# A two-layer hybrid trunk on one core: the norms' last pass put on VectorE, statistics' DMAs issued by ScalarE, leftover attention pieces handed out at another spacing

## The chip, the core and the metric

The kernel runs on one core of a Trainium2 chip, with its five engines: TensorE (PE in the profile, with its weight loads as PEld), VectorE (DVE), ScalarE (ACT), GpSimd (POOL) and SyncE (SP), which issues most DMAs. The metric is the device time of one execution in microseconds; the time of a kernel is the median of its runs.

## The reference, cut to what matters

Two layers over a sequence of 1024 positions and a width of 1024. Layer 0 mixes tokens by dilated sliding-window attention in three head groups, layer 1 by a gated linear recurrence (HGRN2). Behind each mixer stands an MLP. Each of the four sub-layers ends in a LayerNorm of alpha * x + sublayer(x).

```python
def dilated_attention_mixer(x, w_in, w_out):
    proj = (x @ w_in).reshape(B, S, N_GROUPS, 3, ATTN_HEADS, ATTN_HEAD_DIM)
    for g, (window, dilation) in enumerate(((128, 1), (512, 4), (2048, 16))):
        q = rotary(proj[:, :, g, 0], pos)
        k = rotary(proj[:, :, g, 1], pos)
        o, lse = dilated_window_attention(q, k, proj[:, :, g, 2], window, dilation)
        outs.append(o)
        lses.append(lse)
    wts = jax.nn.softmax(jnp.stack(lses, axis=0), axis=0)
    o = jnp.einsum('gbsh,gbshe->bshe', wts, jnp.stack(outs, axis=0))
    return o.reshape(B, S, ATTN_HEADS * ATTN_HEAD_DIM) @ w_out

def squared_relu_mlp(x, w_up, w_down):
    return jnp.square(jax.nn.relu(x @ w_up)) @ w_down

def reference(x, ...):
    for i in range(2):
        y = dilated_attention_mixer(x, ...) if i == 0 else hgrn2_mixer(x, ...)
        x = layer_norm(DEEPNORM_ALPHA * x + y, ln_mix_g[i], ln_mix_b[i])
        y = squared_relu_mlp(x, ffn_w_up[i], ffn_w_down[i])
        x = layer_norm(DEEPNORM_ALPHA * x + y, ln_ffn_g[i], ln_ffn_b[i])
    return x
```

## The kernel before

**Products.** All large products run in split precision: an operand is written as a high part (a rounded copy, made by ACT, line 137) and a low part (the rest, subtracted by DVE, line 138), and three matmuls add up high x high, low x high and high x low. In the names, h and l at the end mark the two parts (woh and wol of the output weights, wh and wl of the recurrent layer's, aoh and aol of the attention's output, d3s of a factor in the MLP).

**Attention.** The projections to q, k and v are computed by 252 steps, in 12 groups of 21, each a product of quarter matrices in a scheme with seven instead of eight products. A group feeds two units; a unit is one pair of heads in one of the three head groups (dilations 16, 4 and 1; eight pairs in all). Unit work is cut in pieces: rotary (line 472 copies by DMA to rot), score products and exponentials (lines 502 to 516), transposes of the probabilities (526, copied to pts by ACT at 529), value products (541, copied to og at 549 or 552). The pieces are put in slots between later projection steps, by tables of numbers; within this part PE and DVE run in exactly the order that the program writes, and so does every engine in its own queue.

**Statistics.** Each unit leaves row maxima and sums in a tile, stats. The function `combine_tr` turns it round on PE (mpt, line 566), copies it to sr (ACT, 569), writes sr to a small array in DRAM, mdram (572), and reads that back in another layout into ml (578 for dilation 1, 581 for the others, where the positions are reordered). Once all three units of a pair are there, `combine` works out the softmax weights over the groups on DVE and ACT (595 to 608), splits them into fh and fl (612, 614), and writes these by six small DMAs into frow (619). `combine_mul` spreads frow over the partitions by a matmul (fb, 629) and weighs the three outputs og with it (630 to 633).

**What is left at the end.** The pieces of the last group, and those whose slots lie past step 252, are packed in 22 lists. `outproj_ln`, which multiplies the attention's output by its output weights and forms the norm, calls `tick()` behind each set of three matmuls; a tick hands out lists in proportion, so that all are out after `ticks` of them (53 for the attention). The first `stage_a` products use the pairs that are ready (nka of them). Earlier pairs lie in DRAM and are read back into onr (875). z is the running sum of a tile of 128 positions, loaded from x at line 911 and finished at 937.

**Norm.** `ln_math` runs over one z tile (128 positions x 1024): statistics (196, 198), subtract the mean and multiply by g (199), the inverse root on small columns (201 to 206), then multiply by it (213, ACT) and add b (214, POOL). The 24 norms of the first three sub-layers end so; the eight of the last one use the branch at 208 to 212, which does both on DVE by halves and stores. The result goes to transposes on PE (lnpt, 223), whose banks ACT and DVE empty into the next operand (233, 234, 291).

There are three PSUM banks for product sums (pmm) and two for transposes. Behind the attention, a scheduler of the framework sets the order on each engine, and inserts the waits; each engine then runs its own queue in order.

Of the kernel before, what the change touches and what calls it, by code (L numbers as in the profile page):

```python
# [9 lines left out]
F32 = mybir.dt.float32  # L10
F32R = mybir.dt.float32r
U8 = mybir.dt.uint8
AF = mybir.ActivationFunctionType
ALU = mybir.AluOpType
AX = mybir.AxisListType

P = 128
# [5 lines left out]
DIL = (1, 4, 16)  # L23
# [39 lines left out]
def trunk_kernel(  # L63
# [24 lines left out]
    nc = tc.nc  # L88
# [16 lines left out]
    act = nc.scalar.activation  # L105
# [87 lines left out]
    def ln_math(z, gB, bB, store=None):  # L193
        st = small([P, 2, 6], "lnst")
        for i in range(2):
            nc.vector.bn_stats(st[:, i], z[:, i * 512:(i + 1) * 512])
        mv = small([P, 2], "lnmv")
        nc.vector.bn_aggr(mv, st)
        nc.vector.scalar_tensor_tensor(z, z, mv[:, 0:1], gB, op0=ALU.subtract, op1=ALU.mult)
        w = small([P, 4], "lnw")  # L200
        act(w[:, 0:1], mv[:, 1:2], AF.Ln, bias=eps_ln)
        act(w[:, 1:2], w[:, 0:1], AF.Exp, scale=-0.5)
        r = w[:, 1:2]
        nc.vector.tensor_scalar(w[:, 2:3], mv[:, 1:2], LN_EPS, r, op0=ALU.add, op1=ALU.mult)
        nc.vector.tensor_scalar(w[:, 2:3], w[:, 2:3], r, -0.5, op0=ALU.mult, op1=ALU.mult)
        nc.vector.tensor_scalar(w[:, 3:4], w[:, 2:3], 1.5, r, op0=ALU.add, op1=ALU.mult)
        if store is not None:
            for i in range(2):
                c = slice(i * 512, i * 512 + 512)
                nc.vector.scalar_tensor_tensor(z[:, c], z[:, c], w[:, 3:4], bB[:, c], op0=ALU.mult, op1=ALU.add)  # L210
                nc.sync.dma_start(store[:, c], z[:, c])
            return
        act(z, z, AF.Copy, scale=w[:, 3:4])  # L213
        nc.gpsimd.tensor_add(z, z, bB)  # L214

    def z_tr(z):

# [104 lines left out]
    def attention(pre, hc):  # L322
# [121 lines left out]
        frow = U("frow", F32R)  # L444
# [119 lines left out]
        def combine_tr(pr, g, slot, ml):  # L564
            pt = bank("pt", "mpt")
            nc.tensor.transpose(pt[:, 0:P], allS, ident)
            q = slice(slot * 32, slot * 32 + 32)
            sr = small([P, P], "sr", 2)
            act(sr[q], pt[q, 0:P], AF.Copy)
            yield  # L570
            md = mdram[pr, g]
            nc.sync.dma_start(md.rearrange("w h (b q) -> (w h b) q", q=P), sr[q])
            yield

            d = DIL[g]
            for w in range(2):
                if d == 1:
                    nc.sync.dma_start(ml[:, w, 0, :], md[w].rearrange("h (i n) -> (h i) n", n=P))
                else:
                    for h in range(2):  # L580
                        nc.sync.dma_start(
                            ml[8 * h:8 * h + 8, w, g, :].rearrange("i (r n) -> i r n", r=d),
# [3 lines left out]
        def combine(pr, ml):  # L586
# [27 lines left out]
            v.tensor_sub(fl, l, fh.bitcast(F32))  # L614
            yield
            for g in range(NG):
                for i, f in enumerate((fh, fl)):
                    r = 4 * g + 2 * i
                    nc.sync.dma_start(frow[r:r + 2, :].bitcast(F32).rearrange("h (i t) -> h i t", t=P),
                                      f[:, g, :].bitcast(F32))  # L620
            yield

        def combine_mul(pr, og, hb):
# [141 lines left out]
        for n in range(len(seq)):  # L765
# [27 lines left out]
            if n % 21 == 14:  # L793
# [25 lines left out]
                                tail[a][0].remove(f)  # L819
        order.__exit__()  # L820
        (ra, ca, sa, _), (rb, cb, sb_, mx) = tail
        done = [f for n in sorted(fill) for f in fill[n]]
        mine = [[ra[0]], [rb[0], rb[1]], [ra[1]], [ca[0], rb[2]], [ca[1]], [cb[0]], [ca[2]], [cb[1]], [ca[3]], [cb[2]],
                [ca[4]] + sa, [cb[3]], [ca[5]], [cb[4]] + sb_, [cb[5]], mx[:1], mx[1:3], mx[3:5], [],
                mx[5:7], mx[7:10], mx[10:]]
        lists = [done[k:k + 1] + (mine[k] if k < len(mine) else []) for k in range(max(len(done), len(mine)))]
        return oN, lists


# [60 lines left out]
    def outproj_ln(pr, oN, fill, resid, gB_ap, bB_ap, keep):  # L890
# [26 lines left out]
        parts = {}  # L917
        total = max(len(fill), 1)
        count = [0, 0]
        ticks = 3 * nka + 5 * 7  # L920

        def tick():
            count[0] += 1
# [840 lines left out]
```

## Time and profile before

| | us |
|---|---|
| three runs | 2829.97, 2828.23, 2829.61 |
| median | 2829.61 |
| profiled execution | 2828.98 |
| its span, first to last instruction | 2827.2 |
| PE busy in it | 2766.7 |
| DVE, ACT, POOL busy | 2069.0, 1450.8, 122.9 |

The granted TensorE clock was 0.997 of full over the span. A row of the timeline reads: start, duration, engine, line, operation, output<-inputs, shape, count of equal rows merged; in brackets the engine's idle time before it and what ended that. A row of the groups has the count, the busy time in all and the mean in nanoseconds of one, and the idle time before it. By forms, a row has the shortest, median and longest duration in nanoseconds.

### The profile page before, as it was taken

The page shows a single profiled execution, that of the slowest core. Times are in us where ns is not written, and L with a number is a line of the kernel's source. Part 1 is how long each engine was busy: PE and PEld are TensorE (multiplying, and loading weights), DVE is VectorE, ACT ScalarE, POOL GpSimd, SP SyncE. Part 2 cuts the span into 40 slices and gives each one's busy share as a digit, 9 for nine tenths or more (in the row PEclk, how much of TensorE's full clock was granted, in tenths as well). Part 3 has the DMA queues.
Part 4 walks back from the last instruction along what each step waited for, and adds up shares of the span by engine and source line. Part 5 has one row for each costly group of instructions (what it writes and reads, how often), then busy time and mean ns, then how long its engine had stood idle before and what let it go on. Part 6 is the DMA issues. An engine that isn't in the chain of part 4 may idle for free.

```text
span 2827.2 us, 40131 instructions
## 1 busy us (share of the span) xinstructions
PE 2766.7 (98%) x14280; PEld 2229.3 (79%) x14280; DVE 2069.0 (73%) x3830; ACT 1450.8 (51%) x3105; POOL 122.9 (4%) x68
## 2 busy tenths in 40 slices
PE   8999999999999989999999999999999999999998
PEld 6777777777777757888878887788887788878887
DVE  7768777777877767786686876565667787678687
ACT  5455555655555555544454444555553644454443
POOL 0000000000000003100000011111102200000000
PEclk9999999999999999999999999999999999999999
DMA  7766665766666523464494752011132355475654
GB/s 286 255 187 208 191 207 173 217 201 198 201 200 220 168 83 134 146 224 160 152 324 127 260 178 98 8 60 60 61 112 104 128 211 176 154 278 188 221 176 130
DMA packets 204936, 485.27 MB, mean 172 GB/s; under 512 B 29376, under 2 KB 43712, under 8 KB 204736
## 3 DMA queue, kind: packets, MB, share of 16 engines
q1 hardware_dynamic: 204736, 482.72, 51.1%
q8 instruction: 112, 1.84, 0.3%
q14 instruction: 88, 0.72, 0.1%
HBM read 362.82 MB, written 94.24 MB: 162 GB/s over the span
## 4 chain that ended last, share of the span: by engine, by line
PE 90%; DVE 5%; ACT 2%; DMA 1%; issue 1%; POOL 0%; SPq 0%; DVEq 0%; POOLq 0%; ACTq 0%
PE pmm L669 8%; PE pmm L671 8%; PE pmm L670 8%; PE pup L1118 7%; PE pup L1116 7%; PE pup L1117 7%; PE pdy L1268 4%; PE pdy L1264 4%; PE pdy L1267 4%; PE s L502 3%; PE pdx L1267 3%; PE pmm L171 3%; PE pdx L1268 3%; PE pmm L173 3%; PE pdx L1264 3%; PE pmm L172 3%
## 5 line engine op out<-in xcount | busy, mean ns | idle before, releaser
L669 PE MATMUL pmm<-xh,H 128*128 128x512 f32 x1008 | 408.5, 405 | 13.2 <-ACT H L432 9.6
L671 PE MATMUL pmm<-xh,H 128*128 128x512 f32 x1008 | 396.5, 393 | 0.2 <-DVE H L440 0.2
L670 PE MATMUL pmm<-xl,H 128*128 128x512 f32 x1008 | 396.0, 393 | 0.0
L669 PEld LDWEIGHTS pmm<-xh,H 128*128 128x128 f32 x1008 | 190.8, 189 | 54.1 <-ACT H L432 9.6
L671 PEld LDWEIGHTS pmm<-xh,H 128*128 128x128 f32 x1008 | 190.4, 189 | 42.6 <-DVE H L440 1.1
L670 PEld LDWEIGHTS pmm<-xl,H 128*128 128x128 f32 x1008 | 191.1, 190 | 36.6
L516 ACT ACTIVATE p<-p,stats 128x128 f32<-128x128 f32 (+1 forms) x384 | 168.3, 441 | 90.7 <-DVE stats L513 89.3
L1264 PE MATMUL pdy<-dT,dS 128*128 128x512 f32 x512 | 199.2, 389 | 0.0
L1267 PE MATMUL pdy<-dT,dS 128*128 128x512 f32 x512 | 199.2, 389 | 0.0
L1268 PE MATMUL pdy<-dT,dS 128*128 128x512 f32 x512 | 199.2, 389 | 0.0
L513 DVE CUSTOM_DVE_ANT_0 p<-s,mask 128x128 f32<-128x128 f32 (+1 forms) x384 | 113.3, 348 | 66.5 <-PE s L502 56.8
L137 ACT ACTIVATE dS<-dr 128x512 fp32r<-128x512 f32 x192 | 119.5, 622 | 73.1 <-PE pdy L1268 36.6
L171 PE MATMUL pmm<-f0nh,wh 128*128 128x512 f32 x384 | 153.1, 399 | 0.0
L173 PE MATMUL pmm<-f0nh,wl 128*128 128x512 f32 x384 | 150.1, 391 | 1.7 <-DVE wl L138 1.6
L172 PE MATMUL pmm<-f0nl,wh 128*128 128x512 f32 x384 | 149.8, 390 | 0.0
L138 DVE TENSOR_TENSOR dS<-dr,dS 128x512 fp32r<-128x512 f32 x192 | 135.4, 705 | 16.2 <-ACT dS L137 14.3
L214 POOL TENSOR_TENSOR z<-z,bB 128x1024 f32<-128x1024 f32 x24 | 58.6, 2444 | 1673.1 <-ACT z L213 1663.0
L529 ACT ACTIVATE pts<-ppt 128x256 f32<-128x256 f32 (+1 forms) x192 | 85.4, 474 | 61.1 <-PE ppt L526 59.0
L137 ACT ACTIVATE dT<-hold 128x512 fp32r<-128x512 f32 x128 | 80.0, 625 | 69.0 <-DVE hold L1243 28.4
L1077 ACT ACTIVATE H<-wc 128x512 fp32r<-128x512 f32 x128 | 77.2, 625 | 73.3 <-DVE wc L1070 43.9
L1267 PEld LDWEIGHTS pdy<-dT,dS 128*128 128x128 f32 x512 | 96.1, 188 | 20.0
L1268 PEld LDWEIGHTS pdy<-dT,dS 128*128 128x128 f32 x512 | 96.1, 188 | 20.0
(396 smaller groups left out, 6946.6 us busy)
## 6 DMA issues: line engine op xcount, KB each, us to landing
xh<-xtd SPq DMA_DIRECT2D x110, 512.0 KB
xl<-xtd SPq DMA_DIRECT2D x110, 512.0 KB
dr<-hd SPq DMA_DIRECT2D x192, 256.0 KB
dr<-in_w_down_dram SPq DMA_DIRECT2D x128, 256.0 KB
rot<-e SPq DMA_DIRECT2D x192, 128.0 KB
wa<-in_w_up_dram SPq DMA_DIRECT2D x48, 512.0 KB
wb<-in_w_attn_dram SPq DMA_DIRECT2D x36, 512.0 KB
wa<-in_w_attn_dram SPq DMA_DIRECT2D x33, 512.0 KB
```

The costliest lines, as they stand in the source:

```text
L137: act(hi, raw, AF.Copy)
L171: nc.tensor.matmul(o, wh[:, k], xs.h(k), start=k == 0, stop=False)
L172: nc.tensor.matmul(o, wh[:, k], xs.l(k), start=False, stop=False)
L173: nc.tensor.matmul(o, wl[:, k], xs.h(k), start=False, stop=k == NK - 1)
L669: nc.tensor.matmul(o, wh, hi[k // 2][:, c], start=begin and k == 0, stop=False, skip_group_check=True)
L670: nc.tensor.matmul(o, wh, lo[k // 2][:, c], start=False, stop=False, skip_group_check=True)
L671: nc.tensor.matmul(o, wl, hi[k // 2][:, c], start=False, stop=end and k == 3, skip_group_check=True)
L1116: nc.tensor.matmul(o, wh, xf.h(b, k), start=begin and k == 0, stop=False, skip_group_check=True)
L1117: nc.tensor.matmul(o, wh, xf.l(b, k), start=False, stop=False, skip_group_check=True)
L1264: nc.tensor.matmul(o[q], h, T_[:, L], start=begin, stop=False, skip_group_check=True)
L1267: nc.tensor.matmul(o[q], h, T_[:, R], start=False, stop=False, skip_group_check=True)
L1268: nc.tensor.matmul(o[q], l, T_[:, L], start=False, stop=end, skip_group_check=True)
```

## The change

It has four parts. The norm's multiply and add become one DVE instruction. In `combine_tr` the write of sr is issued by ACT; for dilation 1 the rows go from sr to ml directly, by two DMAs. In `combine` the three DMAs of fh are issued by ACT, and those of fl stay on SP. The leftover pieces keep their slots' spacing up to a point (slots 0 to 4 as they were, later ones closer), the transposes of the statistics come one list ahead of their DMAs, and the lists are spread over 45 ticks for the attention, not 53.

```diff
@@ ln_math
-        act(z, z, AF.Copy, scale=w[:, 3:4])
-        nc.gpsimd.tensor_add(z, z, bB)
+        nc.vector.scalar_tensor_tensor(z, z, w[:, 3:4], bB, op0=ALU.mult, op1=ALU.add)
@@ combine_tr
-            q = slice(slot * 32, slot * 32 + 32)
+            q0 = slot * 32
             sr = small([P, P], "sr", 2)
-            act(sr[q], pt[q, 0:P], AF.Copy)
+            act(sr[q0:q0 + 32], pt[q0:q0 + 32, 0:P], AF.Copy)
             yield
             md = mdram[pr, g]
-            nc.sync.dma_start(md.rearrange("w h (b q) -> (w h b) q", q=P), sr[q])
+            d = DIL[g]
+            if d == 1:
+                for w in range(2):
+                    nc.scalar.dma_start(ml[:, w, 0, :], sr[q0 + 16 * w:q0 + 16 * w + 16])
+            else:
+                nc.scalar.dma_start(md.rearrange("w h (b q) -> (w h b) q", q=P), sr[q0:q0 + 32])
             yield
 
-            d = DIL[g]
-            for w in range(2):
-                if d == 1:
-                    nc.sync.dma_start(ml[:, w, 0, :], md[w].rearrange("h (i n) -> (h i) n", n=P))
-                else:
+            if d > 1:
+                for w in range(2):
                     for h in range(2):
                         nc.sync.dma_start(
                             ml[8 * h:8 * h + 8, w, g, :].rearrange("i (r n) -> i r n", r=d),
...
@@ combine
             for g in range(NG):
-                for i, f in enumerate((fh, fl)):
+                for i, (f, eng) in enumerate(((fh, nc.scalar), (fl, nc.sync))):
                     r = 4 * g + 2 * i
-                    nc.sync.dma_start(frow[r:r + 2, :].bitcast(F32).rearrange("h (i t) -> h i t", t=P),
-                                      f[:, g, :].bitcast(F32))
+                    eng.dma_start(frow[r:r + 2, :].bitcast(F32).rearrange("h (i t) -> h i t", t=P),
+                                  f[:, g, :].bitcast(F32))
@@ attention, the lists
-        done = [f for n in sorted(fill) for f in fill[n]]
+        done = {}
+        for n in sorted(fill):
+            k = n - len(seq)
+            done.setdefault(k if k < 5 else min(k - 3, 6 + (k - 8) // 2 + (k - 8) % 2), []).extend(fill[n])
-                [ca[4]] + sa, [cb[3]], [ca[5]], [cb[4]] + sb_, [cb[5]], mx[:1], mx[1:3], mx[3:5], [],
+                [ca[4]] + sa[:1], sa[1:] + [cb[3]], [ca[5]], sb_[:1] + [cb[4]], sb_[1:] + [cb[5]], mx[:1], mx[1:3], mx[3:5], [],
-        lists = [done[k:k + 1] + (mine[k] if k < len(mine) else []) for k in range(max(len(done), len(mine)))]
+        lists = [done.get(k, []) + (mine[k] if k < len(mine) else []) for k in range(max(max(done) + 1, len(mine)))]
@@ outproj_ln
-        ticks = 3 * nka + 5 * 7
+        ticks = 3 * nka + 5 * 7 - (8, 0)[pr.mixer]
```

How the order moves is shown at three places. The line numbers of the changed program differ by one to four from those before. First ACT at the end of the attention, where the last pair's statistics leave. Before:

```order
L529 ACTIVATE pts<-ppt 128x512
L569 ACTIVATE sr<-mpt 32x128
L516 ACTIVATE p,stats<-p,stats 128x256 x4
L529 ACTIVATE pts<-ppt 128x512 x2
L552 ACTIVATE og<-o 128x2x256
L137 ACTIVATE aoh<-onr 128x512
L529 ACTIVATE pts<-ppt 128x512 x2
L569 ACTIVATE sr<-mpt 32x128
L137 ACTIVATE aoh<-onr 128x512
L549 ACTIVATE og<-o 128x512
L137 ACTIVATE woh<-wor 128x512 x2
L137 ACTIVATE aoh<-onr 128x512
```

The same place with the change:

```order
L568 ACTIVATE sr<-mpt 32x128
L576 DMA mdram<-sr 32x128
L528 ACTIVATE pts<-ppt 128x512
L515 ACTIVATE p,stats<-p,stats 128x256 x4
L528 ACTIVATE pts<-ppt 128x512 x2
L137 ACTIVATE woh<-wor 128x512 x2
L137 ACTIVATE aoh<-og 128x512
L551 ACTIVATE og<-o 128x2x256
L568 ACTIVATE sr<-mpt 32x128
L528 ACTIVATE pts<-ppt 128x512
L574 DMA ml<-sr 16x128 x2
L528 ACTIVATE pts<-ppt 128x512
```

The last sr now stands ahead of both last pts copies, its two DMAs stand in ACT's queue, and a high part made from og (no load needed) comes ahead of it, where two made from the loaded onr stood.

Second SP, over the same time, from the last long row of frow writes to the load of the norm's weights. Before:

```order
L581 DMA ml<-mdram 8x16x8 x4
L864 DMA wor<-in_w_attn_out_dram 128x512 x2
L911 DMA z<-in_x_dram 128x1024
L875 DMA onr<-ond 128x512
L572 DMA mdram<-sr 32x128
L581 DMA ml<-mdram 8x4x32 x4
L875 DMA onr<-ond 128x512
L911 DMA z<-in_x_dram 128x1024
L572 DMA mdram<-sr 32x128
L864 DMA wor<-in_w_attn_out_dram 128x512 x2
L578 DMA ml<-mdram 16x128 x2
L875 DMA onr<-ond 128x512 x4
```

With the change, from a little earlier:

```order
L915 DMA z<-in_x_dram 128x1024 x3
L471 DMA rot<-e 32x1024 x8
L620 DMA frow<-fl 2x8x128 x3
L582 DMA ml<-mdram 8x16x8 x4
L868 DMA wor<-in_w_attn_out_dram 128x512 x2
L582 DMA ml<-mdram 8x4x32 x4
L915 DMA z<-in_x_dram 128x1024
L879 DMA onr<-ond 128x512 x2
L915 DMA z<-in_x_dram 128x1024
L868 DMA wor<-in_w_attn_out_dram 128x512 x2
L620 DMA frow<-fl 2x8x128 x3
L879 DMA onr<-ond 128x512 x4
```

The writes of mdram and the reads for dilation 1 are gone from SP. The first three z loads stand ahead of the rotary copies and the frow writes (before, one frow write stood ahead of them), and the last four onr loads stand behind the last frow writes.

Third DVE where the first MLP ends and the recurrent layer's products begin, the second-last norm of that stage (f0nl is the low part of the next stage's operand). Before:

```order
L204 TENSOR_SCALAR lnw<-lnmv,lnw 128x1
L234 TENSOR_TENSOR f0nl<-lnpt,f0nh 128x2x128
L205 TENSOR_SCALAR lnw<-lnw 128x1
L206 TENSOR_SCALAR lnw<-lnw 128x1
L138 TENSOR_TENSOR d3s<-d_16021,d3s 128x256
L234 TENSOR_TENSOR f0nl<-lnpt,f0nh 128x2x128 x2
```

With the change:

```order
L204 TENSOR_SCALAR lnw<-lnmv,lnw 128x1
L233 TENSOR_TENSOR f0nl<-lnpt,f0nh 128x2x128
L205 TENSOR_SCALAR lnw<-lnw 128x1
L138 TENSOR_TENSOR d3s<-d_15999,d3s 128x256
L206 TENSOR_SCALAR lnw<-lnw 128x1
L233 TENSOR_TENSOR f0nl<-lnpt,f0nh 128x2x128
L213 SCALAR_TENSOR_TENSOR z<-z,lnw,bB 128x1024
```

The norm's last pass (L213) now stands in DVE's queue two rows behind lnw, ahead of the f0nl rows that follow.

## The prediction

> **What bounds the kernel now.** The page comes first.
>
> ```profile
> span 2827.2 us, 40131 instructions
> PE 2766.7 (98%) x14280; PEld 2229.3 (79%) x14280; DVE 2069.0 (73%) x3830; ACT 1450.8 (51%) x3105; POOL 122.9 (4%) x68
> ```
>
> PE is busy for 2766.7 of 2827.2 us, so some 60 us is all that any edit outside the matmuls can win, and a change in ACT's or DVE's total counts only where PE waits for them. I therefore went through PE's timeline for every wait over a quarter of a microsecond and kept those that the edited code can touch. They lie at three seams, where one stage's norms and the next stage's first products overlap: attention to its output projection (about 975 to 1095 us), the first MLP to the recurrent layer (1726 to 1752), and the second output projection (2173 to 2180).
>
> ```profile
> 985.13 0.50 PE L183 MATMUL pmm<-woh,aoh 128*128 128x512 f32 x1 [1.51 <-DVE z L937]
> 1041.47 0.74 PE L183 MATMUL pmm<-woh,aoh 128*128 128x512 f32 x1 [3.62 <-ACT aoh L137]
> 1051.98 1.19 PE L629 MATMUL fb<-frow,bsel 128*128 128x512 f32 x2 [2.46 <-DMA frow<-fh]
> 1093.25 1.10 PE L223 MATMUL lnpt<-ident,z 128*128 128x128 f32 x8 [0.47 <-issue]
> ...
> 1727.43 0.50 PE L1268 MATMUL pdx<-dT,d3s 128*128 128x512 f32 x1 [1.25 <-DVE d3s L138]
> 1736.19 0.63 PE L223 MATMUL lnpt<-ident,z 128*128 128x128 f32 x4 [2.14 <-DVE f0nl L234]
> 1751.11 0.50 PE L173 MATMUL pmm<-f0nh,wl 128*128 128x512 f32 x1 [1.57 <-DVE wl L138]
> ...
> 2173.91 1.10 PE L223 MATMUL lnpt<-ident,z 128*128 128x128 f32 x8 [0.90 <-issue]
> 2179.86 1.10 PE L223 MATMUL lnpt<-ident,z 128*128 128x128 f32 x8 [0.97 <-issue]
> ```
>
> The brackets add up to 14.9 us. The first four belong to the first seam, the next three to the second, the last two to the third.
>
> **Part 1: the norm's last pass.** It removes 24 ACT multiplies and 24 POOL additions and adds 24 DVE instructions that read two SBUF tensors.
>
> ```profile
> L213 ACT ACTIVATE z<-z,lnw x24: 1138/1152/1157, 1066.7 to 2202.5; 128x1024 f32<-128x1024 f32 x24
> L199 DVE SCALAR_TENSOR_TENSOR z<-z,lnmv,gB x32: 1265/1284/3417, 1063.8 to 2820.3; 128x1024 f32<-128x1024 f32 x32
> L214 POOL TENSOR_TENSOR z<-z,bB 128x1024 f32<-128x1024 f32 x24 | 58.6, 2444 | 1673.1 <-ACT z L213 1663.0
> L199 DVE SCALAR_TENSOR_TENSOR z<-z,lnmv,gB 128x1024 f32<-128x1024 f32 x32 | 48.7, 1522 | 0.5
> ```
>
> The trace has no full-width instruction like the added one, but L199 is of its form, with the same shape and kinds of operands. I take its median, 1.28 us, with 1.27 (its fastest) and 1.52 (its mean) as the ends. Total on DVE: 24 x 1.28 = 30.7 us. ACT loses 24 x 1.15 = 27.6 us, and one norm's chain becomes 1.15 + 2.44 - 1.28 = 2.3 us shorter.
>
> What does the removed POOL addition cost others? Look at the second seam.
>
> ```profile
> 1722.34 4.75 POOL L214 TENSOR_TENSOR z<-z,bB 128x1024 f32<-128x1024 f32 x2 [47.42 <-ACT z L213]
> 1724.82 2.89 DVE L138 TENSOR_TENSOR d3s<-d,d3s 128x256 fp32r<-128x256 f32 x2
> 1733.63 2.08 DVE L138 TENSOR_TENSOR d3s<-d,d3s 128x256 fp32r<-128x256 f32 x1
> 1746.37 1.15 ACT L213 ACTIVATE z<-z,lnw 128x1024 f32<-128x1024 f32 x1 [1.41 <-DVE lnw L206]
> 1747.60 2.38 POOL L214 TENSOR_TENSOR z<-z,bB 128x1024 f32<-128x1024 f32 x1 [11.28 <-ACT z L213]
> 1748.56 2.50 DVE L138 TENSOR_TENSOR wl<-wr,wh 128x1024 fp32r<-128x1024 f32 x1 [2.23 <-ACT wh L137]
> L138 DVE TENSOR_TENSOR d3s<-d,d3s x64: 372/419/2560, 1677.2 to 2815.0; 128x256 fp32r<-128x256 f32 x64
> L138 DVE TENSOR_TENSOR wl<-wr,wh x24: 1202/1226/3051, 1741.6 to 2072.2; 128x1024 fp32r<-128x1024 f32 x24
> ```
>
> Two d3s subtractions that take 0.42 each by the median took 2.89 together while POOL added; one took 2.08; wl took 2.50 instead of 1.23, with POOL's 1747.60 row running across its start. Each time the next PE row is one of the three waits of that seam. So POOL's addition holds up DVE's subtractions, and the waits 1.25 + 2.14 + 1.57 = 4.96 us hang on it (wl's also on L213, which stood 1.15 us ahead of wh on ACT). What is late next is the new instruction itself, now in DVE's queue ahead of the same d3s and f0nl. The first event shows the slack: the excess was 2.89 - 0.84 = 2.05 and PE waited 1.25, so 0.80 was covered. A new pass of 1.28 can leave 1.28 - 0.80 = 0.48 uncovered at d3s and again at f0nl; wl's split runs after wh on ACT, which covers it. I take 4.96 - 0.96 = **4.0 us** gained (ends 2.6, with 0.48 lost five times over, and 5.0).
>
> Third seam and the row at 1093.25: the transposes wait, marked "issue", for a bank that ACT must first empty, and ACT stood in L213.
>
> ```profile
> 2172.18 1.14 ACT L213 ACTIVATE z<-z,lnw 128x1024 f32<-128x1024 f32 x1
> ```
>
> That copy (1.14 us) goes, and each of the three waits (0.90, 0.97, 0.47) is shorter than it: **2.3 us** (ends 0, if the transposes then wait for z on DVE, and 2.3).
>
> Where DVE is already full, its added time could show.
>
> ```profile
> 1060.00:1080.00 20.00, 19.63 (x86) 15.93 (x87) 19.82 (x39) 6.24 (x13) 7.58 (x3) 1.00 0.13 52
> ```
>
> Columns after the length: PE, PEld, DVE, ACT, POOL. DVE is busy 19.82 of 20 us and PE still 19.63, so PE lives off three pmm banks. About six norms finish in this stretch and the ten microseconds behind it: 6 x 1.28 = 7.7, less the 3.42 - 1.28 = 2.1 that the slowest L199 loses to POOL, is 5.5 more on DVE at worst. I take **0.6 lost** (ends 0 and 5.5), since 19.63 against 19.82 says that PE follows DVE only loosely.
>
> A rule to weigh here. SBUF — State Buffer in the Trainium skill (the engine and DMA sides of SBUF, under its diagram) has GpSimd and a DVE instruction with two SBUF inputs share one port pair as an exclusive lock for the whole instruction. The single meetings agree (2.08 for 0.42, against POOL's 2.4). Taken for all 24, the rule would let DVE win back up to 58.6 us for 30.7 paid, and the 0.6 would be a small gain; over all 32 L199 rows the excess is only 32 x (1.52 - 1.28) = 7.7 us, so I stay with the loss.
>
> **Part 2: the statistics' transfers leave SP's queue.** First, why PE waited at 985.13 and 1041.47.
>
> ```profile
> 979.93 0.68 SPq L619 DMA_DIRECT2D frow<-fh  x1
> 980.71 1.29 SPq L911 DMA_DIRECT2D z<-in_x_dram  x3
> ...
> 1033.23 0.27 ACT L569 ACTIVATE sr<-mpt 32x128 f32<-32x128 f32 x1
> 1033.53 0.33 SPq L572 DMA_DIRECT2D mdram<-sr  x1
> 1034.97 0.80 SPq L578 DMA_DIRECT2D ml<-mdram  x2
> 1035.82 1.84 SPq L875 DMA_DIRECT2D onr<-ond  x4
> 1038.67 0.36 DVE L595 TENSOR_TENSOR mn<-ml 16x128 f32<-16x128 f32 x1
> 1045.20 0.52 ACT L612 ACTIVATE fh<-ml 16x384 fp32r<-16x384 f32 x1 [2.73 <-DVE ml L608]
> 1045.75 0.62 SPq L619 DMA_DIRECT2D frow<-fh  x1
> 1046.86 0.61 SPq L619 DMA_DIRECT2D frow<-fl  x1
> 1049.85 0.61 SPq L619 DMA_DIRECT2D frow<-fl  x1
> 1040.00:1060.00 20.00, 14.34 (x42) 9.36 (x42) 15.14 (x29) 4.81 (x10) 0.00 (x0) 0.83 0.29 97
> ```
>
> SP issues in order. The load of z stood behind a frow write that waited for ACT's fh; in the new order the three z loads come first. That wait goes: **1.5 us** (ends 0 and 1.5).
>
> The last pair's statistics are a chain on which PE ends up waiting. From the end of sr (1033.50) to the matmul on frow (1051.98) it takes 18.5 us. Two parts shrink. For the dilation-1 group the detour through DRAM goes: the write's landing lets the read issue 1.44 us after it (1033.53 to 1034.97), so one trip of **1.4** is saved. The six frow writes took from 1045.75 to 1050.46 on one queue. With three on ACT right behind fh, and three on SP from the time at which fl was there (1046.86 in the rows), the last ends near 1046.86 + 3 x 0.61 = 1048.7: **1.8** earlier. Together 3.2 us off the chain. The 3.62 wait (aoh stuck on ACT behind onr loads that stood behind the statistics on SP) should also shrink, and the clock of 0.83 in that window costs up to 20 x 0.17 = 3.4 us. Against it: with 45 instead of 53 ticks the last pieces come at a time with less projection work between them, and PE must wait for their exponentials. Bounds: nothing gained, or 3.62 + 2.46 + 3.4 = 9.5. I take **3.5 us**, beside the 3.2 that the rows of the chain give.
>
> A rule that speaks against this part: DMA: Bandwidth & Descriptors of the Trainium skill (Issuing engines are not separate DMA queues) says that issuing from several engines saves only the sequencer's time to initiate. By it the 1.8 stands, since it is issue time, but the 1.5 at z would not follow; the sum would be that much less. The rows at 979.93 and 980.71 show a wait in line, which the sentence leaves out, so I count it.
>
> The price is on ACT, in all eight pairs.
>
> ```profile
> L529 ACT ACTIVATE pts<-ppt 128x256 f32<-128x256 f32 (+1 forms) x192 | 85.4, 474 | 61.1 <-PE ppt L526 59.0
> 611.63 0.25 ACT L569 ACTIVATE sr<-mpt 32x128 f32<-32x128 f32 x1
> 614.43 0.34 SPq L572 DMA_DIRECT2D mdram<-sr  x1
> ```
>
> No DMA is issued on ACT in this trace, so SP's issue times stand in: per pair 2 x 0.33 for mdram, 2 x 0.40 for ml (1034.97) and 3 x 0.62 for frow, 3.3 us, and for eight pairs 26.6 us. Behind each stand the next pts copies and exponentials, for which PE's value products wait. And the mdram write of 614.43 came 2.55 us after its sr had ended (611.88): SP stood waiting there, and ACT would. But ACT waits for PE, not PE for ACT, in 59.0 us ahead of pts, so most is covered: **1.0 us lost** (ends 0 and 26.6; the 59.0 of cover puts it near the lower).
>
> **Sum**, against the profiled execution's own 2828.98 (span 2827.2, the rest lies around it; 0.63 below the median 2829.61): -4.0 - 2.3 - 1.5 - 3.5 + 0.6 + 1.0 = -9.7, which gives 2819.3 from the profiled execution and 2819.9 from the median. I say **2819.5**.
>
> **Rivals.**
> - The tail gains nothing: the chain is shorter, but the pieces of the last pair now end with nothing else for PE to do, so the wait only moves from frow to the transposes ahead of it. For it: fewer ticks. Against: 3.2 us really leave the chain. Without the 3.5: 2823.0.
> - The tail comes back whole, and the clock stays at 1.00, and neither DVE nor ACT costs PE anything: 2828.98 - 5.0 - 2.3 - 1.5 - 9.5 = 2810.7.
> - **Slower**: ACT's queue becomes the bound of the attention stage. Each DMA instruction is held up there with the copies behind it, so PE's transposes and value products come late step after step. All of the 26.6 us on PE's path: 2819.3 - 1.0 + 26.6 = 2844.9. It decides from the point at which 9.7 + 1.0 = 10.7 of the 26.6 (40%) reach PE; half gives 2831.6. For it: PE and DVE run in a fixed order in that stage, so one late copy holds up all behind it. Against: the 59.0 us of ACT's waiting.
> - The edits cancel or hardly reach PE: POOL's hold is replaced by an equal one on DVE (1.28 each in a full queue, up to 5.5 at 1060 to 1090), the tail gains nothing: 2828.98 - 2.6 - 1.5 + 5.5 = 2830.4. The order of the changed program shows the edits where the diff puts them, so "not done" itself is out.
>
> **How the numbers follow.** A difference within 0.2% (5.7 us, 2824 to 2835) is about what a measurement of this kernel cannot tell from none. Chances: the forecast 0.50 (2815 to 2825), of which 0.04 lies above 2824; the tail without gain 0.22 (2821 to 2827), of which 0.09 is above; the whole tail 0.10; ACT as the bound 0.10, of which 0.08 above 2835; no effect 0.08, of which 0.01 above 2835. That makes faster 0.46 + 0.13 + 0.10 = 0.69, same 0.04 + 0.09 + 0.02 + 0.07 = 0.22, slower 0.09. The range runs from 2809, which takes in the whole tail, to 2828, which takes in the tail without gain and a part of DVE's upper end; left out are ACT as the bound and most of no effect, 0.17.
>
> **What would show it.** Right: no POOL row in the norms; d3s near 0.42 and wl near 1.23 throughout; PE's waits at d3s, f0nl, wl and the three "issue" rows gone or under 0.5; no wait for z near 985; the frow matmul under 16 us after the end of the last sr; PE's waits for pts about as now, with ACT idle ahead of its DMA rows. Wrong: a wait of several us on the last mpt or ppt transposes with a clock below 1 behind it (no gain in the tail); waits for pts and og that grow pair by pair through 200 to 960 us (ACT as the bound); waits on z or pmm at 1060 to 1090 (DVE as the bound). The forecast fails most easily in the tail, where my term is 3.5 between 0 and 9.5.

## The result, and the profile after

| | before | changed |
|---|---|---|
| median of 15 runs each, us | 2828.55 | 2821.91 |
| lowest to highest | 2826.77 to 2831.28 | 2818.93 to 2824.29 |
| profiled execution, us | 2828.98 | 2822.98 |
| its span, us | 2827.2 | 2821.2 |

The ratio is 0.9975 (95% interval 0.9967 to 0.9982): 7.1 us (5.1 to 9.3) faster. The forecast was 2819.5, from a sum of 9.7 faster. The total came out near the sum, but the terms of DVE and of the last pair's statistics did not, and their errors have opposite signs. Two executions in the experiments below, one of 7073 us of the norm alone and one of 3935 us of before beside it, count in no ratio.

The head of the page of the changed kernel:

```profile
span 2821.2 us, 39977 instructions
PE 2766.9 (98%) x14280; PEld 2230.5 (79%) x14280; DVE 2073.4 (73%) x3854; ACT 1425.8 (51%) x3081; POOL 64.5 (2%) x44
```

PE does the same work. DVE has 24 instructions more, but only 4.4 us more to do. The groups by form say why (shortest, median and longest, in ns):

```profile
L213 DVE SCALAR_TENSOR_TENSOR z<-z,lnw,bB x24: 1262/1275/1285, 1069.7 to 2196.8; 128x1024 f32<-128x1024 f32 x24
L199 DVE SCALAR_TENSOR_TENSOR z<-z,lnmv,gB x32: 1265/1280/1286, 1066.3 to 2814.8; 128x1024 f32<-128x1024 f32 x32
L138 DVE TENSOR_TENSOR d3s<-d,d3s x64: 402/416/427, 1674.4 to 2809.4; 128x256 fp32r<-128x256 f32 x64
```

The new pass takes 1.28 us, as its sibling L199 said. The long ones are gone: L199's longest was 3417 and is 1286, d3s had one of 2560 and its longest is 427. 24 x 1.275 = 30.6 us went in, and DVE's busy time grew by only 4.4, so 26.2 us came out elsewhere. Of these, 20.5 can be put to rows: what single rows of before took over the median of their group while a POOL addition of L214 ran (L199 7.7, dS 4.1, d3s 3.8, H 3.6, wl 1.3). With the additions these excesses are gone. Five wl rows of about 3.0 us stay in the recurrent layer, where other work of POOL (L1656) still runs beside them.

To see where the time went, take one matmul after another in both traces (the k-th of its kind in each) and ask how much earlier it starts in the changed kernel. A step of this number is a gain or a loss at that place:

| place, us of before | earlier by | what lies between |
|---|---|---|
| 112 | 0.75 | the start, unchanged code |
| 952 | 1.35 | attention: +0.6 |
| 1150 | 0.12 | first seam: **-1.2** |
| 1690 | 0.22 | first MLP |
| 1762 | 4.35 | second seam: **+4.1** |
| 1830 | 3.30 | start of the recurrent layer: -1.05 |
| 2150 | 3.34 | recurrent layer |
| 2197 | 5.50 | third seam: **+2.2** |
| 2790 | 5.56 | second MLP |

The second and third seams gave what was forecast, and all of the gain. The first seam lost. PE's main waits there from 1030 on, and the one that is left at the second, in the timeline after:

```profile
1030.08 0.73 PE L183 MATMUL pmm<-woh,aoh 128*128 128x512 f32 x2 [0.90 <-ACT aoh L137]
1045.70 0.47 PE L183 MATMUL pmm<-woh,aoh 128*128 128x512 f32 x1 [3.88 <-DVE z L941]
1050.21 1.19 PE L630 MATMUL fb<-frow,bsel 128*128 128x512 f32 x2 [2.71 <-DMA frow<-fl]
1052.30 0.79 PE L183 MATMUL pmm<-woh,aoh 128*128 128x512 f32 x1 [0.89 <-ACT aoh L137]
...
1734.04 0.63 PE L222 MATMUL lnpt<-ident,z 128*128 128x128 f32 x4 [1.43 <-DVE f0nl L233]
```

The wait of 1.51 for z at 985 is gone, and the 3.62 on aoh; in their place stand 3.88 on z (a product bank that DVE had not emptied) and 2.71 on frow, where 2.46 was. The waits at d3s, wl and the three marked "issue" are gone.

Windows in that stretch (PE, PEld, DVE, ACT, POOL with instruction counts, then granted clock, share of the DMA engines busy, GB/s); the first line is of before, the others of the changed kernel:

```profile
1010.00:1030.00 20.00, 19.43 (x142) 13.07 (x140) 11.01 (x41) 16.38 (x52) 0.00 (x0) 1.00 0.20 64
...
1010.00:1030.00 20.00, 16.51 (x120) 10.70 (x118) 10.13 (x37) 14.60 (x47) 0.00 (x0) 1.00 0.02 4
...
1031.00:1034.00 3.00, 2.98 (x36) 2.19 (x37) 0.21 (x1) 1.48 (x4) 0.00 (x0) 1.00 0.97 326
1034.00:1037.00 3.00, 3.00 (x20) 2.37 (x15) 0.48 (x1) 1.12 (x2) 0.00 (x0) 1.00 0.82 310
1037.00:1040.00 3.00, 3.00 (x15) 2.49 (x14) 2.17 (x6) 0.00 (x0) 0.00 (x0) 1.00 0.01 2
```

Two things are to be seen. From 1010 to 1030 PE is busy 16.51 of 20 us, where it was 19.43: the last pieces run with less beside them. From 1031 to 1037 the DMA engines are nearly full (0.97, then 0.82). The chain of the last pair's statistics starts with its transposition on PE, in before at

```profile
1032.35 0.27 PE L566 MATMUL mpt<-ident,stats 128*128 128x128 f32 x1
```

and with the change, put together from the timelines of PE, ACT, SP and DVE:

```profile
1028.04 0.33 PE L565 MATMUL mpt<-ident,stats 128*128 128x128 f32 x1 [0.52 <-ACT pts L528]
1028.37 1.14 ACT L137 ACTIVATE woh<-wor 128x512 fp32r<-128x512 f32 x2
1028.89 0.36 SPq L915 DMA_DIRECT2D z<-in_x_dram  x1
1029.29 0.90 SPq L879 DMA_DIRECT2D onr<-ond  x2
1030.23 0.43 SPq L915 DMA_DIRECT2D z<-in_x_dram  x1
1030.76 0.86 SPq L868 DMA_DIRECT2D wor<-in_w_attn_out_dram  x2
1031.04 0.27 ACT L568 ACTIVATE sr<-mpt 32x128 f32<-32x128 f32 x1
1031.34 1.22 ACTq L574 DMA_DIRECT2D ml<-sr  x2
1037.83 0.38 DVE L596 TENSOR_TENSOR mn<-ml 16x128 f32<-16x128 f32 x1 [3.35 <-DMA ml<-sr]
1044.39 0.52 ACT L613 ACTIVATE fh<-ml 16x384 fp32r<-16x384 f32 x1 [2.75 <-DVE ml L609]
1044.88 0.67 DVE L941 SCALAR_TENSOR_TENSOR z<-z,pmm 128x512 f32<-128x512 f32 x1
```

The transposition started 4.3 us earlier than before (1028.04 for 1032.35), but sr then stood 2.7 us behind other copies on ACT (0.6 before). From the end of sr (1031.31) to the first minimum (mn, on DVE) it took 6.5 us instead of 5.2, though one trip through DRAM was gone: SP, no longer waiting for sr, had just issued its loads. The late minimum is also behind PE's wait of 3.88: the z row that empties the next product bank stands in DVE's queue behind the chain's rows, and starts at 1044.88. The multiplication by frow starts 18.9 us after sr; before it was 18.5. The forecast was 3.2 us less.

### The profile page after: what moved, and what is told of

It is laid out like the page before. It is cut to its first block, busy times and chain, and to the rows that moved or that the text cites. A ratio compares the mean times of both kernels' runs of the same rounds, so it can differ in the third digit from the quotient of the medians.

```text
span 2821.2 us, 39977 instructions
## 1 busy us (share of the span) xinstructions
PE 2766.9 (98%) x14280; PEld 2230.5 (79%) x14280; DVE 2073.4 (73%) x3854; ACT 1425.8 (51%) x3081; POOL 64.5 (2%) x44
## 4 chain that ended last, share of the span: by engine, by line
PE 91%; DVE 5%; ACT 2%; DMA 1%; issue 1%; POOL 0%; SPq 0%; DVEq 0%; ACTq 0%; POOLq 0%
PE pmm L670 8%; PE pmm L672 8%; PE pmm L671 8%; PE pup L1122 7%; PE pup L1120 7%; PE pup L1121 7%; PE pdy L1271 4%; PE pdy L1272 4%; PE pdy L1268 4%; PE pmm L171 3%; PE pdx L1271 3%; PE s L501 3%; PE pdx L1272 3%; PE pmm L172 3%; PE pmm L173 3%; PE pdx L1268 3%
## 5 line engine op out<-in xcount | busy, mean ns | idle before, releaser
L670 PE MATMUL pmm<-xh,H 128*128 128x512 f32 x1008 | 408.2, 405 | 12.9 <-ACT H L431 8.9
L1268 PEld LDWEIGHTS pdy<-dT,dS 128*128 128x128 f32 x512 | 96.1, 188 | 20.1
L1271 PEld LDWEIGHTS pdy<-dT,dS 128*128 128x128 f32 x512 | 96.1, 188 | 19.9
L1272 PEld LDWEIGHTS pdy<-dT,dS 128*128 128x128 f32 x512 | 96.1, 188 | 19.9
```

What stands on the lines that cost most here:

```text
L670: nc.tensor.matmul(o, wh, hi[k // 2][:, c], start=begin and k == 0, stop=False, skip_group_check=True)
L1268: nc.tensor.matmul(o[q], h, T_[:, L], start=begin, stop=False, skip_group_check=True)
L1271: nc.tensor.matmul(o[q], h, T_[:, R], start=False, stop=False, skip_group_check=True)
L1272: nc.tensor.matmul(o[q], l, T_[:, L], start=False, stop=end, skip_group_check=True)
```

## The experiments

Theory A is that of the prediction: the norm gives 5.7 us, the transfers and spacing another 4.0. Theory B is read from the traces: the norm gives all of the gain, and at the first seam the small transfers collide with the loads that SP issues sooner. Theory C: the closer spacing costs the first seam. As a measure beside the time, which scatters by some us from run to run, each run has its **first-seam gain**: how much the products at 1150 us gained on before since those at 952 (the table above: -1.2 for the change). It comes from one trace of each kernel, so it carries what the granted clock did in that one execution; what this does to the comparisons is worked out behind the run with 61 ticks. Ratios are to runs of before beside them, with a 95% interval.

**The norm alone.** Before, with one edit:

```diff
-        act(z, z, AF.Copy, scale=w[:, 3:4])
-        nc.gpsimd.tensor_add(z, z, bB)
+        nc.vector.scalar_tensor_tensor(z, z, w[:, 3:4], bB, op0=ALU.mult, op1=ALU.add)
```

> Before, with the norm's last pass on VectorE alone. Both theories agree here: the waits at d3s, wl and the three bank waits go, so that products are 4.1 us earlier behind the second seam (1760 us) and 2.2 us more behind the third (2200 us); the first seam keeps its waits of 3.6 and 2.5 us, and products at 1122 us stand where they stood (within 0.5). Time 6 us under before, 2822.5. If the norm pass on VectorE were what cost time at the first seam, products at 1122 would be 1 us or more later.

Measured: 2819.26 against 2829.18, ratio 0.9964 (0.9950 to 0.9978). Second seam 4.6, third 2.2, and the first seam gained 1.2, which was not expected. The window there:

```profile
1060.00:1080.00 20.00, 20.00 (x93) 16.52 (x92) 20.00 (x40) 2.38 (x9) 0.00 (x0) 1.00 0.20 79
```

DVE is full for all 20 us and PE does not wait once; before it was 19.63 with POOL busy for 7.58 in the same stretch. The added pass cost DVE less than the holds that went. The norm alone is no slower than the whole change: as far as the times can tell, the rest adds nothing to it.

**All but the norm.** The changed kernel with the two removed lines back:

```diff
-        nc.vector.scalar_tensor_tensor(z, z, w[:, 3:4], bB, op0=ALU.mult, op1=ALU.add)
+        act(z, z, AF.Copy, scale=w[:, 3:4])
+        nc.gpsimd.tensor_add(z, z, bB)
```

> The changed kernel with the norm's last pass as before (ScalarE and GpSimd). Theory A, as predicted: the transfers and the spacing are worth 1.5 + 3.5 - 1.0 = 4.0 us by themselves. Theory B, from the traces: they are worth about nothing, since the first seam as a whole lost 1.2 us and the attention part won 0.6; time within 1.5 us of before.

Measured: 2831.49 against 2829.18, ratio 1.0007 (0.9998 to 1.0016), first-seam gain -3.5. Theory A's 4.0 us for transfers and spacing is out; by the interval they are worth between 0.6 us gained and 4.5 lost, so B's "about nothing" holds at best.

**The transfers undone.** The changed kernel with `combine_tr` and the writes of frow as before:

```diff
-                    nc.scalar.dma_start(ml[:, w, 0, :], sr[q0 + 16 * w:q0 + 16 * w + 16])
+            nc.sync.dma_start(md.rearrange("w h (b q) -> (w h b) q", q=P), sr[q])
...
-                for i, (f, eng) in enumerate(((fh, nc.scalar), (fl, nc.sync))):
+                for i, f in enumerate((fh, fl)):
```

> The changed kernel with the statistics' transfers as before (all on SyncE, through DRAM), with the new norm and spacing. Theory A: the last pair's chain is 3.2 us longer than in the changed kernel, 3 to 5 us slower than it. Theory B: SyncE waits for the statistics again and so holds its large loads back, the chain from sr to the first minimum is back at about 5.2 us from 6.5, and the time is within 2 us of the changed kernel or under it.

Measured: 2827.64 against 2829.18, ratio 0.9992 (0.9984 to 1.0001), first-seam gain -5.2. This speaks for A and against B: with the new spacing the new transfers are worth 4 us at the seam (-5.2 to -1.2), and the time agrees (the intervals do not meet). But it isn't A's longer chain: from sr to the multiplication by frow it takes 18.7 us for 18.9. sr itself ends 5.4 us later, at 1036.69.

**The spacing undone.** The changed kernel with `done`, `mine` and `lists` as before, and 53 ticks:

```diff
-            done.setdefault(k if k < 5 else min(k - 3, 6 + (k - 8) // 2 + (k - 8) % 2), []).extend(fill[n])
+        done = [f for n in sorted(fill) for f in fill[n]]
...
-                [ca[4]] + sa[:1], sa[1:] + [cb[3]], [ca[5]], sb_[:1] + [cb[4]], sb_[1:] + [cb[5]], mx[:1], mx[1:3], mx[3:5], [],
+                [ca[4]] + sa, [cb[3]], [ca[5]], [cb[4]] + sb_, [cb[5]], mx[:1], mx[1:3], mx[3:5], [],
...
-        ticks = 3 * nka + 5 * 7 - (8, 0)[pr.mixer]
+        ticks = 3 * nka + 5 * 7
```

> The changed kernel with the leftover pieces spaced as before and 53 ticks. Theory A: within 1.5 us of the changed kernel. Theory B: the loads still collide with the last statistics (over 5 us from sr to the first minimum), time within 2 us of the changed kernel. Theory C, that the closer spacing and not the transfers cost the first seam: 2 us or more faster than the changed kernel.

Measured: 2820.96 against 2829.18, ratio 0.9971 (0.9960 to 0.9981), first-seam gain +1.1, that is 2.3 better than the change. From sr to the first minimum it takes 5.2 us. By time, nothing is told apart from the changed kernel; by the seam, theory C gains. Against the norm alone (+1.2) the transfers are worth nothing under the old spacing.

**Ticks alone.** One number:

```diff
-        ticks = 3 * nka + 5 * 7 - (8, 0)[pr.mixer]
+        ticks = 3 * nka + 5 * 7
```

> The changed kernel with 53 ticks in place of 45. Theory C (fewer projection steps between the pieces cost the first seam): the waits of 0.3 to 0.9 us between 1010 and 1030 us go, 2 us or more faster than the changed kernel. Theory B (the transfers' late landing decides): within 1.5 us of the changed kernel.

Measured: 2817.90 against 2829.19, ratio 0.9962 (0.9949 to 0.9976), first-seam gain **+4.5**, 5.7 us better than with 45. In its windows and timeline:

```profile
1010.00:1030.00 20.00, 19.45 (x141) 13.56 (x143) 12.35 (x40) 16.04 (x49) 0.00 (x0) 1.00 0.04 10
```

PE is busy 19.45 of 20 us where it was 16.51. In the order of the program, 144 products of the output projection stand ahead of the last transposed statistics, with 45 ticks 126: 18 products of 0.23 us, 4.1 us of work that filled waits on pts and stats, and still that transpose starts only 0.9 us later (1028.97 for 1028.04). That the 45 ticks took 2.9 us of PE's work from this stretch is shown, and so theory C for that part; the rest of the 5.7 is looked at below. By time, the run is 4.0 us under the changed kernel in the medians, but the intervals overlap.

**53 ticks, all transfers as before.** The edits of the last run and of "the transfers undone" together.

> New norm, new spacing, 53 ticks, all the statistics' transfers as before on SyncE. It says what the transfers are worth where the ticks do no harm. If they help by themselves, the first seam gains 2 us or more less than in the run with 53 ticks and the new transfers (4.5); if the ticks alone were the matter, within 1 us of it.

Measured: 2826.33 against 2828.85, ratio 0.9991 (0.9982 to 0.9999), first-seam gain -4.7. So the table for the first seam, all with the new norm, is:

| lists and ticks | transfers as before | new transfers |
|---|---|---|
| old lists, 53 | +1.2 | +1.1 |
| new lists, 53 | -4.7 | +4.5 |
| new lists, 45 | -5.2 | -1.2 |

The new lists lose with the old transfers and don't with the new ones (9.2 us between the two cells of the middle row; in time 0.9991 and 0.9962), the new transfers do nothing without the new lists, and with the new transfers the 45 ticks lose against 53, by 5.7 us in this measure. By time, the best cell (0.9962) is not told apart from the norm alone (0.9964). In the run with the old transfers the last mpt starts at 1037.28, 8.3 us later than with the new ones, with six more products ahead of it; which of SP's waits sets it back was not tried.

**The collision.** The changed kernel with loads near the last statistics cut to 64 columns: two z loads to a sixteenth, the second halves of the onr loads to an eighth. The kernel leaves out the values of the other columns (they are set to zero); it was run once, in 2818.94 us:

```diff
-                nc.sync.dma_start(zt, resid(len(z)))
+                if pr.mixer == 0 and len(z) in (3, 4):
+                    nc.sync.dma_start(zt[:, :64], resid(len(z))[:, :64])
+                    nc.gpsimd.memset(zt[:, 64:], 0.0)
+                else:
+                    nc.sync.dma_start(zt, resid(len(z)))
...
+            if self.mixer == 0 and h == 1:
+                nc.sync.dma_start(self.raw[k][:, c][:, :64], oN[k][:, c][:, :64])
+                nc.gpsimd.memset(self.raw[k][:, c][:, 64:], 0.0)
+            else:
+                nc.sync.dma_start(self.raw[k][:, c], oN[k][:, c])
```

> The changed kernel with the two later z loads and the second halves of the onr loads cut to 64 columns, the rest of those tiles set to zero by GpSimd (so the values of those parts are left out). Some 1 MB less is in flight when the last pair's statistics go from sr to ml. Theory B (the small transfer lands late because SyncE's large loads are in flight): the first minimum starts 3 to 4.5 us after the end of sr, not 6.5. Rival D (a direct transfer issued by ScalarE is slow by itself): still 6 us or more.

Measured: 3.3 us from the end of sr to the first minimum, not 6.5.

```profile
1029.02 0.27 ACT L568 ACTIVATE sr<-mpt 32x128 f32<-32x128 f32 x1
1029.31 1.22 ACTq L574 DMA_DIRECT2D ml<-sr  x2
1032.63 0.38 DVE L596 TENSOR_TENSOR mn<-ml 16x128 f32<-16x128 f32 x1 [0.17 <-DMA ml<-sr]
```

and in the windows of that run:

```profile
1029.00:1032.00 3.00, 2.98 (x36) 2.21 (x37) 0.23 (x1) 1.98 (x4) 0.00 (x0) 1.00 0.70 207
1032.00:1035.00 3.00, 3.00 (x18) 2.37 (x15) 2.83 (x8) 0.60 (x1) 0.00 (x0) 1.00 0.08 16
```

The same two transfers from the same queue are through in half the time when less is in flight. In both runs the minimum follows as the engines fall quiet: here at 1032.63, with a share of 0.70 in the 3 us ahead of 1032 and 0.08 behind it; in the change at 1037.83, with 0.97 and 0.82 up to 1037 and 0.01 behind. So the collision is shown, in one trace, and the transfer is not slow by itself. The first-seam gain is +1.9, 3.1 us better than the change; that is a rougher number, since the order of the products behind the first multiplication by frow differs a little there.

**Through DRAM again.** The changed kernel with the dilation-1 rows written to mdram by ACT and read by SP:

```diff
-                    nc.scalar.dma_start(ml[:, w, 0, :], sr[q0 + 16 * w:q0 + 16 * w + 16])
+            nc.scalar.dma_start(md.rearrange("w h (b q) -> (w h b) q", q=P), sr[q0:q0 + 32])
...
+                    nc.sync.dma_start(ml[:, w, 0, :], md[w].rearrange("h (i n) -> (h i) n", n=P))
```

> The changed kernel with the dilation-1 statistics through DRAM again (write issued by ScalarE, reads by SyncE). By the prediction's term the detour costs 1.4 us of chain, so 8 us from sr to the first minimum and 1 to 1.5 us more time. Theory B: the reads stand in SyncE's queue and hold the loads behind them back, so sr to the first minimum is 5 to 6.5 us and the time within 1.5 us of the changed kernel, on either side.

Measured: 2820.59 against 2829.19, ratio 0.9970 (0.9959 to 0.9981), 5.6 us from sr to the first minimum, first-seam gain +0.9. The detour was quicker than the direct way. In the order of that program the reads stand on SP ahead of an onr, a z and two wor loads, which went out from 1034.28 on; in the changed kernel all of them were out by 1031.62. With 53 ticks it was tried again:

> 53 ticks, dilation-1 statistics through DRAM with the reads on SyncE. At 45 ticks the detour was 2.2 us better at the first seam (0.94 gained against 1.23 lost). If that is general, the seam gains 5.5 us or more here; if it came from the loads that the reads held back there, it is within 1 us of the direct way's 4.5, on either side.

Measured: 2818.26 against 2828.85, ratio 0.9962 (0.9948 to 0.9976), first-seam gain +2.7, now 1.8 less than the direct way, with 5.8 us from sr to the first minimum for 5.2. Neither expectation held, and these runs don't say which way is better in general; what the clock has in the 1.8 is shown below.

**The chain's head freed.** sr copied by VectorE, the dilation-1 rows sent by SP:

```diff
-            act(sr[q0:q0 + 32], pt[q0:q0 + 32, 0:P], AF.Copy)
+            nc.vector.tensor_copy(sr[q0:q0 + 32], pt[q0:q0 + 32, 0:P])
...
-                    nc.scalar.dma_start(ml[:, w, 0, :], sr[q0 + 16 * w:q0 + 16 * w + 16])
+                    nc.sync.dma_start(ml[:, w, 0, :], sr[q0 + 16 * w:q0 + 16 * w + 16])
```

> The changed kernel with sr copied by VectorE and its dilation-1 rows sent to ml by SyncE, which in the order then stand ahead of the two z and the onr loads. Theory B (the last statistics lose 2.1 us in ScalarE's queue and 1.4 us or more behind the loads): sr ends within 0.8 us of the transposed statistics instead of 3.3, the first minimum starts 2.5 to 4 us after sr instead of 6.5, the multiplication by frow starts 4 us earlier, and the time is 2 to 5 us under the changed kernel. Rival: the loads held back come too late for z and onr and give it back; time within 1.5 us of it, with PE waiting for z or aoh.

Measured: 2818.49 against 2829.19, ratio 0.9965 (0.9952 to 0.9977), first-seam gain +1.6.

```profile
1029.85 0.30 DVE L568 COPY sr<-mpt 32x128 f32<-32x128 f32 x1 [1.68 <-PE mpt L565]
1032.31 0.37 DVE L596 TENSOR_TENSOR mn<-ml 16x128 f32<-16x128 f32 x1
1044.81 0.70 PE L630 MATMUL fb<-frow,bsel 128*128 128x512 f32 x2 [0.31 <-DMA frow<-fl]
```

and in its windows:

```profile
1050.00:1060.00 10.00, 9.19 (x19) 5.56 (x19) 8.18 (x14) 3.34 (x6) 0.00 (x0) 0.50 0.45 162
```

sr to the first minimum is 2.2 us and the multiplication by frow starts 5.4 us earlier, but the seam gains only 2.8 on the change; the clock of 0.50 in the ten microseconds behind, and a wait of 1.99 us for og, stand against it. With 53 ticks the two do not add up:

> 53 ticks, sr copied by VectorE, the dilation-1 rows sent by SyncE. If the two gains at the first seam add up (5.7 from the ticks, 2.8 from sr and SyncE, each against the changed kernel by the place of the products at 1150 us), products there are 7 us or more earlier against those at 952 than in before; if both fill the same wait, 4 to 5. Time 2 to 4 us under the run with 53 ticks, or equal to it.

Measured: 2818.68 against 2828.85, ratio 0.9964 (0.9951 to 0.9976), first-seam gain +2.7, less than the ticks alone: PE waits 5.78 us for one high part on ACT, which there stands behind woh (2.68 us of waiting for its load), fh and the three frow writes (2.04 us of issuing). Neither expectation for the seam held; the time is level with the run with 53 ticks.

**61 ticks.**

```diff
-        ticks = 3 * nka + 5 * 7 - (8, 0)[pr.mixer]
+        ticks = 3 * nka + 5 * 7 + (8, 0)[pr.mixer]
```

> The changed kernel with 61 ticks. If the seam's loss goes with how few projection products lie between the pieces, 61 is as good as 53 or better (first seam 4.5 us or more gained); rival: the last pieces then end with no products left beside them, the wait for frow comes back, and the gain is 2 us or more smaller.

Measured: 2816.55 against 2828.85, ratio 0.9958 (0.9946 to 0.9971), first-seam gain +4.8. It is the fastest median of all, level with 53 ticks and with the norm alone by the intervals, and its interval just touches that of the change (0.9967 to 0.9982).

**What the clock has in these gains.** PE's idle time between 975 and 1100 us (125 less its busy time in that window) and the granted clock from 1040 to 1065, where it drops at this seam, in the same traces:

| run | first-seam gain | PE idle, us | clock |
|---|---|---|---|
| before | 0 | 11.8 | 0.86 |
| norm alone | +1.2 | 9.9 | 0.80 |
| the change (new lists, 45) | -1.2 | 12.9 | 0.80 |
| old lists, 53 | +1.1 | 10.1 | 0.80 |
| new lists, 53 | +4.5 | 9.8 | 0.93 |
| new lists, 61 | +4.8 | 9.1 | 0.93 |
| new lists, 53, transfers as before | -4.7 | 14.9 | 0.73 |
| chain's head freed, 45 | +1.6 | 7.8 | 0.73 |
| chain's head freed, 53 | +2.7 | 10.0 | 0.80 |
| through DRAM, 53 | +2.7 | 7.2 | 0.66 |

The windows of the change, of 53 ticks and of the freed head:

```profile
975.00:1100.00 125.00, 112.15 (x585) 82.24 (x583) 91.32 (x207) 48.70 (x138) 0.00 (x0) 0.96 0.23 77
1040.00:1065.00 25.00, 16.03 (x51) 9.99 (x50) 19.98 (x36) 6.81 (x12) 0.00 (x0) 0.80 0.32 108
...
975.00:1100.00 125.00, 115.21 (x615) 85.13 (x614) 95.28 (x215) 52.59 (x146) 0.00 (x0) 0.99 0.28 95
1040.00:1065.00 25.00, 17.91 (x63) 12.03 (x63) 21.41 (x40) 4.64 (x10) 0.00 (x0) 0.93 0.22 76
...
975.00:1100.00 125.00, 117.17 (x604) 86.21 (x602) 94.53 (x214) 51.34 (x142) 0.00 (x0) 0.95 0.27 86
1040.00:1065.00 25.00, 20.89 (x59) 12.98 (x58) 17.68 (x30) 6.82 (x13) 0.00 (x0) 0.73 0.39 129
```

From the change to 53 ticks PE waits 3.1 us less; a clock of 0.93 for 0.80 over 25 us is worth up to another 25 x 0.13 = 3.3 us (an estimate, for a PE that is busy throughout). From the change to the freed head it waits 5.0 us less, and up to 25 x 0.07 = 1.8 us go to the clock. The two are not independent, since a slow PE also has less left to wait for, but the gains of 5.7 and 2.8 don't rank these edits. Nor do the times: the trace of 53 ticks is of an execution of 2815.22 us, for a median of 2817.90, that of the freed head of one of 2820.07, for a median of 2818.49, and the medians lie 0.6 us apart. In the same way, new lists with 53 ticks make PE wait hardly less than the old lists (9.8 for 10.1); their 3.4 us more at the seam go with the clock. And through DRAM with 53 ticks PE waits less than the direct way (7.2 for 9.8), at the lower clock (0.66 for 0.93). Whether an edit decides the clock there, or chance, was not tried.

## Why the prediction was right or wrong

- **Second seam** (4.0 forecast): right in mechanism and size, 4.1 gained. d3s and wl lost their holds; the new pass ahead of f0nl left 1.43 us, where twice 0.48 had been allowed.
- **Third seam** (2.3 forecast with the row at 1093): right. The two waits went (2.2); the one at 1093 went too.
- **DVE as it fills up** (0.6 lost): wrong in sign. The step that failed counted the holds that go only in L199's excess, 7.7 us. 26.2 us came back, since d3s, dS, H and wl were held too, and with the norm alone PE waited 1.9 us less at the first seam (9.9 for 11.8). The rule of SBUF — State Buffer in the Trainium skill (SBUF: two separate sides), one port pair locked for a whole instruction between GpSimd and such a DVE instruction, bounded it at 58.6 and was the better guide: it said that this term might be a gain.
- **The wait for z** (1.5): it went, as said, wherever the new transfers stand (in the runs with the old ones it is 1.8 to 1.9 at that place). The rule weighed there, of DMA: Bandwidth & Descriptors in the Trainium skill (Issuing engines are not separate DMA queues), would have left it out; the measurement decides.
- **The last pair's statistics** (3.5 gained, between 0 and 9.5): wrong, the main error. Two steps failed. "One trip of 1.4 is saved" priced the landing by before, where the DMA engines were busy for 0.33 of 1033 to 1036 (0.97 and 0.82 behind sr after); freed of its wait, SP issued 2 MB of loads between 1028.89 and 1031.62 and the first minimum came 6.5 us behind sr, 3.2 us more than with small loads. And the 45 ticks, named in the prediction as what stands against it but not priced, took 2.9 us of PE's work between 1010 and 1030 (4.0 us in the medians against 53 ticks, with intervals that overlap). The sign given for a right forecast, the frow matmul under 16 us after sr, failed at 18.9. The 1.8 saved at frow was 1.0 (fh's end to the multiplication 5.3 us for 6.3).
- **ACT's queue in the attention** (1.0 lost): no loss shows. PE's waits for pts stayed at 0.47 each, and all its waits from 200 to 960 us add up to 5.8 us (6.0 before). The 0.6 gained there is within the scatter of the runs that issue transfers on ACT too (from 1.4 lost to 2.2 gained between 112 and 952 us). The rival in which ACT becomes the bound is out. At the end of the attention, though, ACT's order did hold sr for 2.7 us.
- **The sum**: the norm was undervalued (5.7 forecast; 8.0 by its three seams when alone, 1.2 + 4.6 + 2.2), the rest overvalued (4.0 gained forecast, 2 us lost by the run without the norm, with an interval from 0.6 gained to 4.5 lost). That the total came so near is luck as far as these two errors cancel. Of the rivals, the tail without gain (2823.0) was the nearest in mechanism, though the largest wait moved to z and not to the transposes.

## What to carry to other kernels

Taking a wait off a queue also sets free what stood behind it: ask which loads now start earlier, and whose small transfers they will meet in the DMA engines. When a gain between two places of a trace is used to rank edits, take it apart into waits and clock first, and ask whether the profiled execution was a typical one: here 5.7 us against 2.8 turned into 3.1 us of waits against 5.0. When parts of a change are tied to each other, run all four combinations of two of them, since here the new transfers alone were worth nothing and the new lists alone a loss. And run the simplest part by itself: the norm alone did as well as the whole.

## What the runs showed of the hardware that was not expected

The granted clock after a short stall is not the same from run to run. In all fourteen traces PE stops for 2.09 us, beginning between 113.9 and 117.5 us, in the same products. Windows behind it, of before and then of the norm alone (the seventh number is the clock):

```profile
116.00:120.00 4.00, 1.91 (x17) 1.28 (x16) 1.07 (x2) 2.55 (x5) 0.00 (x0) 1.00 1.02 410
120.00:124.00 4.00, 4.00 (x12) 3.10 (x11) 0.00 (x0) 1.57 (x4) 0.00 (x0) 0.58 0.67 268
```

```profile
116.00:120.00 4.00, 1.91 (x17) 1.35 (x16) 0.69 (x1) 2.97 (x6) 0.00 (x0) 1.00 1.03 418
120.00:124.00 4.00, 4.00 (x26) 3.01 (x25) 0.60 (x5) 2.18 (x6) 0.00 (x0) 1.00 0.54 217
```

One drops to 0.58 behind the stop, the other stays at 1.00; the second gains 1.6 us on the first between 112 and 252 us. In nine of the fourteen the clock drops there, in five it does not. The loss of 1.05 us at the start of the recurrent layer is of the same kind: a wait of 1.27 us stands there in both kernels, and the clock from 1805 to 1825 was

```profile
1805.00:1825.00 20.00, 19.06 (x109) 15.27 (x110) 15.57 (x30) 11.05 (x17) 4.72 (x2) 0.91 0.00 1
```

in the changed kernel and 1.00 in before. What decides it was not tried. A single trace of this kernel therefore carries 1 to 2 us at each such place that belong to no edit that is known; gains are better read from place to place than from the span, and beside the clock of the place.
